# VectorE in place of GpSimd for weight and input splits of a hybrid decoder step, and a new order of TensorE's steps

## Chip, core and metric

The kernel runs on one core of one Trainium2 chip. The metric is the device time of one execution in microseconds; a comparison takes the median of several executions. The engines are named as in the profile: PE (TensorE, with its weight loads as PEld), DVE (VectorE), ACT (ScalarE), POOL (GpSimd), SP (SyncE, which issues most DMAs).

## What is computed

One layer of a decoder for a prompt of 512 rows and 8 single-row samples (520 columns in all once transposed), width 1024, all in float32:

```
h = rms_norm(x, g_mix)
proj = einsum('ntd,de->nte', h, w_in)                  # 5632 columns
u_a, z_b, u_c, gate_in = split(proj)                   # 1024, 1024, 512, 3 x 1024
c_a = causal_dwconv(u_a, width 4)                      # branch A: RG-LRU
y_a = linear_scan(a, sqrt(1 - a*a) * sigmoid(ig) * c_a)  # gates by 8 block-diagonal products
glu_b = z_b[:512] * sigmoid(z_b[512:])                 # branch B: Conformer convolution
y_b = silu(layer_norm(causal_dwconv(glu_b, width 31)))
y_c = s5_ssm(u_c)                                      # branch C: complex diagonal scan
y_c = gelu(y_c); y_c = y_c * sigmoid(y_c @ w_glu_c + b)
merged = g_a * (y_a @ w_pa) + g_b * (y_b @ w_pb) + g_c * (y_c @ w_pc)
x = x + merged @ w_out
x = x + (silu(gate) * up) @ w_ffn_out                  # gate, up = rms_norm(x) @ w_ffn_in
out = rms_norm(x, g_final), and the new states of all branches
```

## The kernel before

Activations lie transposed: 128 channels on the partitions, the 520 columns on the free axis in two halves of 260. Every large product is made from split operands: a float32 operand is divided into a high part (`hi`, rounded by ScalarE's copy) and a low part (`lo = x - hi`), and three products hi.hi, hi.lo, lo.hi are summed in PSUM (`prod`, L252). An output tile of 128 channels with 8 input tiles is therefore 48 TensorE instructions, one with 4 input tiles 24.

Weights come in by SP's DMAs of 1024 KB (two output tiles at a time, `wload`), two such buffers. `wsplit` makes `whi` on ScalarE (L226) and `wlo` by a subtraction (L227); there are three buffers of each, so the split for one product waits until the product three weights earlier is done. Which engine subtracts is a table: `eng(key)` gives GpSimd for the keys in ON_POOL and VectorE for the others. Weight keys are `w.<matrix>.<tile>`, for instance `w.in.23`; tiles 0 to 7 of w_in are step a, 8 to 11 b1, 12 to 15 b0, 20 to 27 ga, 28 to 35 gb, 36 to 43 gc. Other keys: `ac.t` the split of branch A's convolved input (in `a_conv`, helper `split`, L258 and L259), `ya.t` the split of its output, `yg.k` the split after the GELU, `wrg.t` that of the gate weights, `rot.t` and `unrot.t` the imaginary half of the rotations before and after the S5 scan (L917 to L919, L927 to L929), `eb`, `ca` (L840 to L848), `wt` (L810 to L820) tables of branch C, `caz`, `ebz` memsets, `hs.t` the 8 sample columns of the RG-LRU state (L1125 to L1131). ON_DVE does the same for `ca` and `wt`, whose default is GpSimd.

The order of the middle part is the string ORDER, written out by hand. Each word calls one step function: b0/b1 (branch B's two halves of the input product), a (branch A's), gc/ga/gb (the gates, stored to DRAM as g_d and loaded back), cp/cq/cr/cd/cm/ci/co (branch C: tables, transposes, products, scan, output), ac (branch A's width-4 convolution, L1057 to L1067), ag (its gate products, two tiles' weights fetched at every even one), ar (its recurrence, in pairs), bc (branch B's width-31 convolution), glu, pc/pa/pb (the three output projections), ln1 to ln3. TensorE executes in exactly this order. The other four engines' queues are laid out by the framework's scheduler from the same sequence, and each engine executes its queue in order. `b_low` emits branch B's convolution with a very low priority: its 29 multiply-adds per tile (L1229, two dependent chains `acc` and `odd`) fill VectorE's queue where nothing more urgent stands.

After ORDER follow w_out with the residual, the FFN in two halves, the last norm and the stores.

Of the kernel before, what the change touches and what calls it, by code (L numbers as in the profile page):

```python
# [29 lines left out]
DFF = 2816  # L30

ON_POOL = set("""
ac.0 ac.4 ac.6 ac.7 caz.0 caz.1 caz.2 eb.1 ebz.0 ebz.1 ebz.2 ebz.3 hs.0 hs.2 hs.3 hs.4 hs.5 hs.6 hs.7 rho.2
rot.1 rot.2 rot.3 unrot.3 w.glu.0 w.glu.1 w.glu.3 w.in.10 w.in.12 w.in.2 w.in.21 w.in.23 w.in.26 w.in.31 w.in.35
w.in.37 w.in.38 w.in.39 w.in.4 w.in.40 w.in.7 w.in.8 w.w_pa.1 w.w_pa.3 w.w_pa.4 w.w_pa.5 w.w_pa.7 w.w_pb.1
w.w_pb.2 w.w_pb.5 w.w_pb.7 w.w_pc.0 w.w_pc.2 w.w_pc.3 w.w_pc.5 w.w_pc.6 w.w_pc.7 wrg.6 ya.1 ya.2 yg.0 yg.3
""".split())

ON_DVE = set("""
ca.2 ca.3 wt.0 wt.1 wt.3  # L40
""".split())

CONV_PE = ()
AFTER3 = False

ORDER = """
b0.0 cp.0 as b0.1 ct ap s0 bs cp.1 b1.0 b1.1 cr.0 b0.2 cq.1 b0.3 ci.0 cr.1 gc.0 gc.1 cq.0 b1.2 cd.0 b1.3 cm.0 a.0 ci.1
a.2 ac.0 a.1 cd.1 a.3 a.4 ac.1 gc.2 co.0 cp.2 gc.3 cm.1 cr.2 ag.0 cq.2 co.1 cd.2 ag.1 ac.2 ci.2 a.5 cp.3 ac.3 gc.4
gc.5 cm.2 cr.3 co.2 cd.3 ag.2 ar.0 gc.6 gc.7 cq.3 ci.3 cm.3 ga.0 ga.1 ag.3 ga.6 ga.7 a.6 a.7 bc.0 ac.4 ac.5 ar.1 ga.2
ga.3 ag.4 ag.5 bc.1 ar.2 bc.2 ga.4 ga.5 co.3 gb.4 ac.6 gb.5 gelu ag.6 glu.0 glu.1 ac.7 glu.2 glu.3 gb.0 gb.1 ag.7 pc.0  # L50
pc.1 ar.3 pc.2 bc.3 pc.3 asp pc.4 pc.5 gb.2 pc.6 pc.7 gb.3 lnp pa.0 pa.1 pa.2 pa.3 ln1 gb.6 gb.7 ln2 pa.4 pa.5 pa.6
ln3 pa.7 pb.0 pb.1 pb.2 pb.3 pb.4 pb.5 pb.6 pb.7
"""


# [1576 lines left out]
```

## Time and profile before

| what | value |
|---|---|
| median of 3 runs | 929.35 us (928.15 to 930.03) |
| profiled execution | 928.63 us |
| its span, first to last instruction | 926.6 us |
| PE busy | 866.2 us, 93% of the span, 7329 instructions |
| DVE busy | 598.2 us, 65%, 942 |
| ACT busy | 355.1 us, 38%, 519 |
| POOL busy | 299.2 us, 32%, 363 |
| mean granted TensorE clock | 0.97 |
| weight splits on DVE (L227) | 113, 128.0 us |
| weight splits on POOL (L227) | 33, 77.7 us, mean 2355 ns |

Busy shares are averages over stages with different limits, so the table only says where to look. The views that decide are those of one stage: the busy time of each engine in a stretch, what an engine waited for there, and the mean of one instruction beside its undisturbed duration.

### The profile page before, as it was taken

The page shows a single profiled execution, that of the slowest core. Times are in us where ns is not written, and L with a number is a line of the kernel's source. Part 1 is how long each engine was busy: PE and PEld are TensorE (multiplying, and loading weights), DVE is VectorE, ACT ScalarE, POOL GpSimd, SP SyncE. Part 2 cuts the span into 40 slices and gives each one's busy share as a digit, 9 for nine tenths or more (in the row PEclk, how much of TensorE's full clock was granted, in tenths as well). Part 3 has the DMA queues.
Part 4 walks back from the last instruction along what each step waited for, and adds up shares of the span by engine and source line. Part 5 has one row for each costly group of instructions (what it writes and reads, how often), then busy time and mean ns, then how long its engine had stood idle before and what let it go on. Part 6 is the DMA issues. An engine that isn't in the chain of part 4 may idle for free.

```text
span 926.6 us, 17538 instructions
## 1 busy us (share of the span) xinstructions
PE 866.2 (93%) x7329; PEld 854.6 (92%) x7329; DVE 598.2 (65%) x942; ACT 355.1 (38%) x519; POOL 299.2 (32%) x363
## 2 busy tenths in 40 slices
PE   7879999979968589899999999999999999999997
PEld 6879999879968579799999999999999999999997
DVE  7897877797799999997784454444432234444443
ACT  6523243436466546334443443333221223333331
POOL 6558987746845754424311200000000000000021
PEclk9989999999998879899999999999999999999999
DMA  6921333232312304453454222322133432321322
GB/s 198 281 89 58 115 105 112 73 93 81 126 57 69 104 23 150 160 183 105 160 204 140 92 90 90 123 92 72 52 87 92 147 109 92 104 71 43 98 75 92
DMA packets 103630, 99.74 MB, mean 108 GB/s; under 512 B 8675, under 2 KB 94935, under 8 KB 103023
## 3 DMA queue, kind: packets, MB, share of 16 engines
q1 hardware_dynamic: 103215, 98.01, 32.4%
q8 instruction: 57, 0.93, 0.4%
q0 software_dynamic: 320, 0.57, 0.2%
q14 instruction: 22, 0.18, 0.1%
q10 hardware_dynamic: 16, 0.03, 0.0%
HBM read 86.57 MB, written 12.58 MB: 107 GB/s over the span
## 4 chain that ended last, share of the span: by engine, by line
PE 76%; DVE 16%; POOL 3%; issue 2%; ACT 1%; DMA 1%; SPq 0%; DVEq 0%; ACTq 0%; POOLq 0%
PE mm L252 69%; DVE t L1229 4%; PE mm L1581 3%; DVE q L1229 2%; DVE wlo L227 1%; PE mm L969 1%; DMA t<-w_ig 1%; DVE tx L1059 1%; DVE s_t L592 1%; PE mm L905 1%; DMA q<-x_prompt 1%; DVE s_n L601 1%; DVE h L259 1%; DVE q L1129 0%; POOL h L352 0%
## 5 line engine op out<-in xcount | busy, mean ns | idle before, releaser
L252 PE MATMUL mm<-q,whi 128*128 128x260 f32 x3296 | 420.4, 285 | 5.2 <-ACT t L138 2.3
L252 PEld LDWEIGHTS mm<-q,whi 128*128 128x128 f32 x3296 | 406.9, 190 | 7.2 <-ACT t L138 2.9
L227 DVE TENSOR_TENSOR wlo<-wraw,whi 128x1024 fp32r<-128x1024 f32 (+3 forms) x113 | 128.0, 1133 | 231.3 <-PE mm L252 130.4
L226 ACT ACTIVATE whi<-wraw 128x1024 fp32r<-128x1024 f32 (+3 forms) x146 | 139.4, 955 | 245.9 <-PE mm L252 213.1
L252 PE MATMUL mm<-q,wlo 128*128 128x260 f32 x1648 | 215.4, 282 | 0.0
L252 PEld LDWEIGHTS mm<-q,wlo 128*128 128x128 f32 x1648 | 204.5, 188 | 0.0
L1453 POOL TENSOR_TENSOR t<-t,t 128x260 f32<-128x260 f32 (+1 forms) x9 | 8.4, 931 | 370.5 <-ACT t L1451 370.5
L252 PE MATMUL mm<-h,whi 128*128 128x260 f32 x800 | 108.2, 290 | 4.4 <-DVE h L259 3.6
L252 PEld LDWEIGHTS mm<-h,whi 128*128 128x128 f32 x800 | 103.1, 196 | 5.4 <-DVE h L259 4.2
L227 POOL TENSOR_TENSOR wlo<-wraw,whi 128x1024 fp32r<-128x1024 f32 (+1 forms) x33 | 77.7, 2355 | 69.7 <-ACT whi L226 26.4
L1229 DVE SCALAR_TENSOR_TENSOR t<-q,vec,t 128x512 f32<-128x512 f32 x71 | 61.4, 883 | 0.0
L252 PE MATMUL mm<-h,wlo 128*128 128x260 f32 x400 | 57.1, 289 | 4.0 <-DVE wlo L227 4.0
L252 PEld LDWEIGHTS mm<-h,wlo 128*128 128x128 f32 x400 | 52.8, 194 | 4.3 <-DVE wlo L227 4.3
L138 ACT ACTIVATE t<-t,zero_t 128x520 f32<-128x520 f32 x30 | 21.5, 729 | 56.6 <-DVE t L1522 56.6
L252 PE MATMUL mm<-t,t 128*128 128x260 f32 x96 | 17.3, 338 | 24.8 <-ACT t L258 24.1
L252 PEld LDWEIGHTS mm<-t,t 128*128 128x128 f32 x96 | 15.2, 235 | 26.6 <-ACT t L258 25.0
L138 ACT ACTIVATE t<-mm,vec 128x520 f32<-128x520 f32 x44 | 30.0, 689 | 19.6 <-PE mm L252 16.5
L1229 DVE SCALAR_TENSOR_TENSOR q<-q,vec 128x512 f32<-128x512 f32 x30 | 31.0, 1035 | 0.0
L132 ACT ACT_TABLE_LOAD x22 | 28.2, 1283 | 1.1 <-PEq L1620 0.7
L258 ACT ACTIVATE h<-t 128x520 fp32r<-128x520 f32 x18 | 11.5, 636 | 43.8 <-DVE t L592 43.8
L1372 POOL TENSOR_TENSOR t<-t,t 128x520 f32<-128x520 f32 x7 | 9.2, 1318 | 50.0 <-ACT t L1371 50.0
L592 DVE TENSOR_TENSOR t<-t,t 128x520 f32<-128x520 f32 x30 | 20.8, 699 | 0.7
(424 smaller groups left out, 980.5 us busy)
## 6 DMA issues: line engine op xcount, KB each, us to landing
wraw<-w_ffn_in SPq DMA_DIRECT2D x22, 1024.0 KB
wraw<-w_in SPq DMA_DIRECT2D x20, 1024.0 KB
g_d<-t SPq DMA_DIRECT2D x24, 260.0 KB
t<-g_d SPq DMA_DIRECT2D x24, 260.0 KB
wraw<-w_ffn_out SPq DMA_DIRECT2D x16, 384.0 KB
wraw<-w_ffn_out SPq DMA_DIRECT2D x16, 320.0 KB
wraw<-w_pa SPq DMA_DIRECT2D x4, 1024.0 KB
wraw<-w_out SPq DMA_DIRECT2D x4, 1024.0 KB
```

The lines of the kernel that those rows point to most:

```text
L132: last_tab[0] = after(S.preload_act_table_set(SETS[func]), last_tab[0])
L138: last_tab[0] = after(S.activation(out, x, func, **kw), last_tab[0])
L226: S.activation(hi, raw, AF.Copy)
L227: e.tensor_tensor(lo, raw, hi.bitcast(F32), op=ALU.subtract)
L252: T.matmul(ps[:, h, 0:HN], w_, x[:, h * HN:(h + 1) * HN], start=first and i == 0, stop=last and i == n - 1)
L258: S.activation(hi, src, AF.Copy)
L259: e.tensor_tensor(lo, src, hi.bitcast(F32), op=ALU.subtract)
L592: V.tensor_tensor(out, x, y, op=ALU.mult)
L601: V.tensor_scalar(n_, n_, MG, None, op0=ALU.subtract)
L905: T.matmul(ps[:, q // 2, (q % 2) * 136:(q % 2) * 136 + 136], d["ebt"][:, ri, q, :], d["u4"][:, q, 8:144], start=True, stop=True)
L1229: ins = V.scalar_tensor_tensor(x, win(k), wdw(k, t), x, op0=ALU.mult, op1=ALU.add)
L1581: T.matmul(ps[:, 0, 0:HN], w[:, k, :], x[:, h * HN:(h + 1) * HN], start=j == 0 and k == 0 and i == 0, stop=j == 1 and k == hk - 1 and i == 2)
```

## The change

Two tables and the string are edited; no instruction's arithmetic changes. Twenty weight splits move from GpSimd to VectorE (w_in tiles 7, 12, 21, 23, 26, 31, 35, 37, 38; glu 0, 1; pa 1, 4, 7; pb 5; pc 2, 3, 5, 6, 7) and four the other way (w_in 36, w_out 3, pa 2, pb 4). ac.0, ac.4, ac.6, ac.7, ya.2, rot.2, rot.3, unrot.3, hs.3, hs.7 and three memsets (caz.0 to caz.2) move to VectorE, yg.2 and caz.3 to GpSimd. The tables ca.0 and wt.2 move to VectorE. In ORDER some 30 of 131 steps stand elsewhere: among them a.6 before ga.6 and ga.7, ac.4 before ci.3, bc.0 before a.6, bc.2 before ar.2, bc.3 right behind ag.6, co.3 right behind ag.5, and ga.4, ga.5 and ag.7 behind pc.1. Line numbers of the changed file are one lower from L52 on.

```
 ON_DVE = set("""
-ca.2 ca.3 wt.0 wt.1 wt.3
+ca.0 ca.2 ca.3 wt.0 wt.1 wt.2 wt.3
 """.split())
...
-gc.5 cm.2 cr.3 co.2 cd.3 ag.2 ar.0 gc.6 gc.7 cq.3 ci.3 cm.3 ga.0 ga.1 ag.3 ga.6 ga.7 a.6 a.7 bc.0 ac.4 ac.5 ar.1 ga.2
-ga.3 ag.4 ag.5 bc.1 ar.2 bc.2 ga.4 ga.5 co.3 gb.4 ac.6 gb.5 gelu ag.6 glu.0 glu.1 ac.7 glu.2 glu.3 gb.0 gb.1 ag.7 pc.0
+gc.5 cm.2 cr.3 co.2 cd.3 ag.2 ar.0 gc.6 gc.7 ag.3 cm.3 cq.3 ac.4 ci.3 ga.0 ga.1 bc.0 a.6 ga.6 ga.7 a.7 ac.5 ar.1 ga.2
+ga.3 ag.4 ag.5 co.3 bc.1 bc.2 ar.2 gb.4 ac.6 gb.5 gelu ag.6 bc.3 glu.0 glu.1 ac.7 glu.2 glu.3 gb.0 gb.1 pc.0 pc.1 ga.4
```

VectorE's queue where branch B's convolution begins, before. `wlo` is a weight split (here for a.6, then ga.2), L1202 to L1236 the sample columns of the convolution, L1229 its multiply-adds, L1061 and L1067 the end of ac.4, L1059 a part of ac.5:

```order
L227 TENSOR_TENSOR wlo_3262<-wraw_3259,whi_3261 128x1024
L227 TENSOR_TENSOR wlo_3471<-wraw_3468,whi_3470 128x1024
L1202 TENSOR_TENSOR t_3372<-q_801,vec 128x248
L1206 TENSOR_REDUCE t_3374<-t_3372 128x8
L1061 SCALAR_TENSOR_TENSOR t_3414<-q_804,vec,tx_3410 128x2x256
L1067 SCALAR_TENSOR_TENSOR t_3414<-q_804,vec,tx_3410 128x2x4
L1236 TENSOR_SCALAR t_3371<-t_3374,vec 128x2x4
L1229 SCALAR_TENSOR_TENSOR t_3371<-q_801,vec,t_3371 128x2x256
```

And in the changed kernel (L926 to L928 are unrot.3; the two splits are those for ga.7 and a.7):

```order
L927 TENSOR_TENSOR t_3016<-t_3010,h_2540 128x512
L591 TENSOR_TENSOR h_2996<-t_3011,h_2540 128x4x128
L926 TENSOR_TENSOR t_3015<-t_3011,h_2540 128x512
L226 TENSOR_TENSOR wlo_3313<-wraw_3254,whi_3312 128x1024
L1201 TENSOR_TENSOR t_3159<-q_801,vec 128x248
L924 TENSOR_TENSOR h_3009<-h_2996 128x4x128
L928 TENSOR_TENSOR h_3009<-t_3015,t_3016 128x4x128
L1205 TENSOR_REDUCE t_3161<-t_3159 128x8
L1235 TENSOR_SCALAR t_3158<-t_3161,vec 128x2x4
L226 TENSOR_TENSOR wlo_3369<-wraw_3197,whi_3368 128x1024
L1228 SCALAR_TENSOR_TENSOR t_3158<-q_801,vec,t_3158 128x2x256
```

The convolution's first multiply-add stood behind the split for ga.2 and now stands behind the one for a.7, two steps earlier in TensorE's order; unrot.3 and a.7's split, which were GpSimd's, stand ahead of it.

GpSimd's queue from the GELU to the w_pc products, before (L259 are the splits of ac.6, wrg.6, yg.0, yg.3, ac.7, ya.1, ya.2; L1118 multiplications of the recurrence; L227 the weight splits of glu and pc):

```order
L259 TENSOR_TENSOR t_3967<-t_3963,t_3966 128x520
L259 TENSOR_TENSOR t_4047<-t_4045,t_4046 128x512
L259 TENSOR_TENSOR h_4029<-q_607,h_4028 128x520
L259 TENSOR_TENSOR h_4031<-q_607,h_4030 128x520
L1118 TENSOR_TENSOR t_4069<-t_4069,t_3963 128x520
L227 TENSOR_TENSOR wlo_4195<-wraw_4158,whi_4194 128x512
L259 TENSOR_TENSOR t_4151<-t_4147,t_4150 128x520
L227 TENSOR_TENSOR wlo_4370<-wraw_4367,whi_4369 128x512
L259 TENSOR_TENSOR h_4568<-q_803,h_4567 128x520
L259 TENSOR_TENSOR h_4570<-q_803,h_4569 128x520
L227 TENSOR_TENSOR wlo_4468<-wraw_4465,whi_4467 128x512
L1118 TENSOR_TENSOR t_4358<-t_4358,t_4147 128x520
```

And in the changed kernel:

```order
L258 TENSOR_TENSOR t_3933<-t_3931,t_3932 128x512
L258 TENSOR_TENSOR h_3915<-q_607,h_3914 128x520
L258 TENSOR_TENSOR h_3917<-q_607,h_3916 128x520 x2
L1131 COPY fin_a<-q_804 128x1
L1117 TENSOR_TENSOR t_3955<-t_3955,t_3849 128x520
L1131 COPY fin_a<-q_804 128x1
L226 TENSOR_TENSOR wlo_4119<-wraw_4082,whi_4118 128x512
L226 TENSOR_TENSOR wlo_4276<-wraw_4273,whi_4275 128x512
L258 TENSOR_TENSOR h_4635<-q_803,h_4634 128x520
L1117 TENSOR_TENSOR t_4411<-t_4411,t_4071 128x520
```

The splits of ac.6, ac.7, ya.2 and of pc.2 are gone from it, and one more GELU split (yg.2) is in it.

## Rows read from the trace of the kernel before

**Rows 1.** Busy time by stretch: a:b, length, PE, PEld, DVE, ACT, POOL, PEclk, DMA, GB/s.
```profile
45.00:250.00 205.00, 193.34 (x1811) 188.03 (x1810) 160.84 (x316) 80.38 (x127) 149.78 (x220) 0.97 0.29 93
250.00:402.00 152.00, 119.53 (x981) 117.25 (x981) 149.66 (x191) 83.11 (x115) 79.16 (x58) 0.89 0.30 102
402.00:485.00 83.00, 83.00 (x687) 82.76 (x687) 68.08 (x78) 33.40 (x44) 24.97 (x13) 1.00 0.45 158
```
**Rows 2.** Timeline of PE at pa.0: start, length, engine, line, what.
```profile
402.06 4.00 PE L252 MATMUL mm<-h,whi 128*128 128x260 f32 x32
```
**Rows 3.** What PE waited for from 245 to 333 us: total, times, longest.
```profile
PE mm L252 <- ACT t L258: 21.2, 2, 11.4
PE mm L252 <- DVE h L259: 3.6, 1, 3.6
```
**Rows 4.** DVE by line and form, 250.2 to 402: busy us, mean ns, idle before.
```profile
L1229 DVE SCALAR_TENSOR_TENSOR t<-q,vec,t 128x512 f32<-128x512 f32 x66 | 57.7, 894 | 0.0
L1229 DVE SCALAR_TENSOR_TENSOR q<-q,vec 128x512 f32<-128x512 f32 x24 | 24.5, 1020 | 0.0
L1229 DVE SCALAR_TENSOR_TENSOR q<-q,vec,q 128x512 f32<-128x512 f32 x15 | 14.2, 946 | 0.2
L227 DVE TENSOR_TENSOR wlo<-wraw,whi 128x1024 fp32r<-128x1024 f32 x8 | 9.7, 1209 | 0.0
L1059 DVE SCALAR_TENSOR_TENSOR tx<-q,vec,tx 128x544 f32<-128x544 f32 x6 | 6.8, 1129 | 0.0
...
L227 DVE TENSOR_TENSOR wlo<-wraw,whi 128x512 fp32r<-128x512 f32 x3 | 2.0, 671 | 0.0
```
**Rows 5.** Line L1229: shortest, median, longest ns over the trace.
```profile
L1229 DVE SCALAR_TENSOR_TENSOR t<-q,vec,t x71: 718/740/2887, 250.3 to 414.3; 128x512 f32<-128x512 f32 x71
```
**Rows 6.** Timeline, 252 to 258 us, DVE and POOL.
```profile
252.87 2.83 POOL L227 TENSOR_TENSOR wlo<-wraw,whi 128x1024 fp32r<-128x1024 f32 x1
253.38 2.91 DVE L1059 SCALAR_TENSOR_TENSOR tx<-q,vec,tx 128x544 f32<-128x544 f32 x1
...
257.54 0.77 DVE L1059 SCALAR_TENSOR_TENSOR tx<-q,vec,tx 128x544 f32<-128x544 f32 x1
```
**Rows 7.** POOL by line and form, 250.2 to 402.
```profile
L227 POOL TENSOR_TENSOR wlo<-wraw,whi 128x512 fp32r<-128x512 f32 x9 | 20.1, 2236 | 14.3 <-issue 9.1 <-ACT whi L226 4.2 <-PE mm L252 0.9
L259 POOL TENSOR_TENSOR t<-t,t 128x520 fp32r<-128x520 f32 x3 | 11.2, 3748 | 9.5 <-ACT t L258 9.5
L227 POOL TENSOR_TENSOR wlo<-wraw,whi 128x1024 fp32r<-128x1024 f32 x3 | 8.8, 2926 | 7.4 <-ACT whi L226 7.4
...
L259 POOL TENSOR_TENSOR h<-q,h 128x520 fp32r<-128x520 f32 x4 | 6.6, 1658 | 2.9 <-ACT h L258 2.9
L1118 POOL TENSOR_TENSOR t<-t,t 128x520 f32<-128x520 f32 x4 | 5.8, 1449 | 1.2 <-ACT t L138 1.2
```
**Rows 8.** Timeline: PE's last products of ag.3; DVE where the convolution begins.
```profile
233.78 1.47 PE L252 MATMUL mm<-t,t 128*128 128x260 f32 x11
...
246.84 1.57 DVE L227 TENSOR_TENSOR wlo<-wraw,whi 128x1024 fp32r<-128x1024 f32 x1 [4.99 <-PE mm L252]
...
250.30 3.15 DVE L1229 SCALAR_TENSOR_TENSOR t<-q,vec,t 128x512 f32<-128x512 f32 x3
```
**Rows 9.** DVE by line, 45 to 250.2: the group with most idle before it.
```profile
L227 DVE TENSOR_TENSOR wlo<-wraw,whi 128x1024 fp32r<-128x1024 f32 x16 | 21.3, 1332 | 21.2 <-PE mm L252 11.2 <-ACT whi L226 9.9
```
**Rows 10.** What PE waited for from 160 to 210 us.
```profile
PE ms L859 <- DVE h L789: 3.0, 1, 3.0
```
**Rows 11.** Timeline, 270 to 282 us: a weight split's high part, then ag.4's gate weights.
```profile
270.65 1.06 ACT L226 ACTIVATE whi<-wraw 128x1024 fp32r<-128x1024 f32 x1
...
280.43 0.63 ACT L258 ACTIVATE t<-t 128x512 fp32r<-128x512 f32 x1 [6.62 <-DMA t<-w_ig]
281.09 0.69 DVE L259 TENSOR_TENSOR t<-t,t 128x512 fp32r<-128x512 f32 x1 [1.70 <-ACT t L258]
```
**Rows 12.** Timeline: PE at glu.0.
```profile
332.71 2.94 PE L252 MATMUL mm<-h,whi 128*128 128x260 f32 x10 [3.56 <-DVE h L259]
```

More of the change, by code (lines that the diff above doesn't have):

```diff
@@ L32 @@
 ON_POOL = set("""
[L33 to L36, printed above, removed]
+caz.3 eb.1 ebz.0 ebz.1 ebz.2 ebz.3 hs.0 hs.2 hs.4 hs.5 hs.6 rho.2 rot.1 w.glu.3 w.in.10 w.in.2 w.in.36 w.in.39 w.in.4
+w.in.40 w.in.8 w.w_out.3 w.w_pa.2 w.w_pa.3 w.w_pa.5 w.w_pb.1 w.w_pb.2 w.w_pb.4 w.w_pb.7 w.w_pc.0 wrg.6 ya.1 yg.0 yg.2
+yg.3
 """.split())
 ON_DVE = set("""
-ca.2 ca.3 wt.0 wt.1 wt.3
+ca.0 ca.2 ca.3 wt.0 wt.1 wt.2 wt.3
 """.split())
@@ L46 @@
 ORDER = """
-b0.0 cp.0 as b0.1 ct ap s0 bs cp.1 b1.0 b1.1 cr.0 b0.2 cq.1 b0.3 ci.0 cr.1 gc.0 gc.1 cq.0 b1.2 cd.0 b1.3 cm.0 a.0 ci.1
-a.2 ac.0 a.1 cd.1 a.3 a.4 ac.1 gc.2 co.0 cp.2 gc.3 cm.1 cr.2 ag.0 cq.2 co.1 cd.2 ag.1 ac.2 ci.2 a.5 cp.3 ac.3 gc.4
-gc.5 cm.2 cr.3 co.2 cd.3 ag.2 ar.0 gc.6 gc.7 cq.3 ci.3 cm.3 ga.0 ga.1 ag.3 ga.6 ga.7 a.6 a.7 bc.0 ac.4 ac.5 ar.1 ga.2
-ga.3 ag.4 ag.5 bc.1 ar.2 bc.2 ga.4 ga.5 co.3 gb.4 ac.6 gb.5 gelu ag.6 glu.0 glu.1 ac.7 glu.2 glu.3 gb.0 gb.1 ag.7 pc.0
-pc.1 ar.3 pc.2 bc.3 pc.3 asp pc.4 pc.5 gb.2 pc.6 pc.7 gb.3 lnp pa.0 pa.1 pa.2 pa.3 ln1 gb.6 gb.7 ln2 pa.4 pa.5 pa.6
-ln3 pa.7 pb.0 pb.1 pb.2 pb.3 pb.4 pb.5 pb.6 pb.7
+b0.0 cp.0 as b0.1 ct s0 bs cp.1 b1.0 b1.1 cr.0 b0.2 b0.3 cq.1 ci.0 cr.1 gc.0 gc.1 b1.2 cd.1 cd.0 b1.3 a.0 cq.0 cm.0
+ci.1 a.2 a.1 a.3 ac.1 gc.2 a.4 ac.0 cp.2 co.0 gc.3 cd.2 cm.1 ap ag.0 cq.2 co.1 ac.2 cr.2 ag.1 ci.2 a.5 cp.3 ac.3 gc.4
+gc.5 cm.2 cr.3 co.2 cd.3 ag.2 ar.0 gc.6 gc.7 ag.3 cm.3 cq.3 ac.4 ci.3 ga.0 ga.1 bc.0 a.6 ga.6 ga.7 a.7 ac.5 ar.1 ga.2
+ga.3 ag.4 ag.5 co.3 bc.1 bc.2 ar.2 gb.4 ac.6 gb.5 gelu ag.6 bc.3 glu.0 glu.1 ac.7 glu.2 glu.3 gb.0 gb.1 pc.0 pc.1 ga.4
+ag.7 ga.5 ar.3 pc.2 pc.3 pc.4 pc.5 asp gb.2 pc.6 pc.7 gb.3 lnp pa.0 pa.1 pa.2 pa.3 ln1 gb.6 gb.7 ln2 pa.4 ln3 pa.5
+pa.6 pa.7 pb.0 pb.1 pb.2 pb.3 pb.4 pb.5 pb.6 pb.7
 """
```

## Prediction

> **What bounds the kernel now.** Read the stages first [rows 1]. From 45 to 250 us TensorE (PE) is busy 193.34 of 205 us and VectorE (DVE) 160.84, so TensorE sets the pace and VectorE has 44.2 us to spare. From 250 to 402 us it is the other way round: VectorE is busy 149.66 of 152 us, TensorE only 119.53, at a granted clock of 0.89. From 402 to 485 us TensorE is busy 83.00 of 83 us, and behind that stand w_out and the FFN, of which the change moves one split. So the stretch up to the first w_pa product, pa.0, which starts at 402.06 us [rows 2], is what can move.
>
> Then ask what TensorE waits for in the middle [rows 3]: 21.2 us in two waits, for ScalarE rows that themselves stand behind VectorE work, and 3.6 us for a VectorE split directly. They are one lateness, met at several steps: VectorE's queue is too long.
>
> Then ask what fills that queue. The depthwise convolution (L1229) is 66+24+15 instructions with means of 894, 1020 and 946 ns [rows 4], but the median of the first form, over its 71 in the whole trace, is 740 ns and its longest is 2887 [rows 5]. The timeline shows why [rows 6]: the same L1059 instruction takes 2.91 us beside a weight split that runs on GpSimd (POOL) and 0.77 us four microseconds later, when GpSimd runs no tensor_tensor. A long GpSimd tensor_tensor stops one VectorE instruction for a while; VectorE pays for work that it was spared.
>
> **What one GpSimd instruction costs VectorE.** Over the stretch, mean against undisturbed: 66 x (894-740) = 10.2 us, 24 x (1020-740) = 6.7, 15 x (946-740) = 3.1, the six L1059 6 x (1129-770) = 2.2; 22.2 us, a lower bound, since the smaller groups are left out. On the other side stand GpSimd's long instructions [rows 7]: 9 of 512 columns, 3+4+4 of 520 and 3 of 1024; counted in units of about 512 columns 9+11+6 = 26. That is 0.85 us a unit at least; the pair in [rows 6] shows 2.91-0.77 = 2.14 for a split of two units, 1.07 each. I take **1.0 us a unit**, between the two. It can't be less than nothing, nor more than such an instruction itself takes, 1.45 us (the L1118 rows of [rows 7]).
>
> By the Trainium skill's page "SBUF — State Buffer" (section "A bandwidth-pool intuition that's wrong (but worth ruling out)") two such operations don't share a bandwidth: one is blocked until the other ends. By that rule a unit would cost the whole of GpSimd's time, the upper bound of 1.45, and the gain would be 7.2 us larger; the pair says 1.07, so the trace agrees with a block and not with its length, and the sum stays with 1.0.
>
> **The change, part by part.**
>
> *The middle stretch.* Off GpSimd go seven 512-column splits (glu.0, glu.1, pc.2, pc.3, pc.5, pc.6, pc.7), three of 1024 (in.23, in.31, pa.1), the input splits ac.4, ac.6 and ac.7, and ya.2; yg.2 comes the other way. Units: 7+6+4-1 = 16, relief 16.0 us. VectorE's own price, duration less about 0.08 us by which neighbours overlap (1.21 for 1024 and 0.67 for 512 columns [rows 4], 0.69 for 520 [rows 11]): 3 x 1.13 + 7 x 0.59 + 3 x 0.61 = 9.35 us. **Net 6.65 us less** in a queue that has no idle time. Bounds: no relief makes it 9.35 us more, 1.45 a unit 13.9 us less.
>
> *The start of the convolution.* It begins at 250.30 us, behind the split for ga.2, for which VectorE stood idle 4.99 us until TensorE had done ga.7 [rows 8]. In the new order it stands behind the split for a.7, whose buffer comes free when a.6 is done, and a.6 now follows directly on the steps that end with ag.3 today, at 235.25 us [rows 8]. With a step of 48 products at 48 x 83.00/687 = 5.8 us [rows 1], ScalarE's part at 1.06 [rows 11] and the split at 1.21, that is 243.3 us: up to 7.0 us earlier, if VectorE has done what stands ahead. Ahead of it VectorE gets five splits of 1024 net (in.12, 37, 38, 21, 26 and 7 come, in.36 goes): 5.65 us; rot.2, rot.3 and unrot.3 with three instructions each, wt.2 with six, and ac.0: 16 x 0.61 = 9.8; ca.0 with eight smaller ones at half that, 2.6. Together 18.1 us, less a relief of up to 10+16+4 = 30 units if all collided and nothing if none did. Of the 44.2 us idle there, 21.2 are splits that wait for TensorE's pace [rows 9], a wait that shrinks as VectorE gets later. So I let this cover hide the 18.1 us. Where the cover fails is known: TensorE waits 3.0 us for c_pool's rows there now (L789 [rows 10]), and that would grow first. I take **5 us earlier**, between 7 and a loss of 2.
>
> *New or kept waits.* The gate weights of ag.4 are still fetched only when GpSimd's small state copies have freed their tile: then comes a DMA that ScalarE waits 6.62 us for, and 1.70 us of VectorE idle [rows 11]. hs.4 stays on GpSimd, so this chain stays; with the shorter queue VectorE waits more there, some 3 us. The split for pc.3 now waits for ga.4, which stands only three steps ahead of it: about 1 us. Together **2.1 us worse** than now.
>
> *TensorE's order.* ga.4 and ga.5 move from before co.3 to behind pc.1. They are fillers of 5.8 us each; moved, they leave TensorE less to do before ag.6 and glu.0, and more behind. From glu.0 to pa.0 TensorE then has 12 steps of 24 products, 6 of 48 and one pair of gates: 34.8+34.8+1.4 = 71 us. For pa.0 at 392.6 glu.0 must run from 321.6 on. Its last wait ends today at 332.71 us [rows 12], 11 us too late; but that time holds the 11.6 us of ga.4 and ga.5, and VectorE's share of the gain, so this fits with a few us to spare. I cost it at nothing; without that room pa.0 is late by what is missing.
>
> *Everything else.* SP's queue moves with the steps (weights and gates are issued at the same distance ahead). pa.2, w_out.3 and pb.4 go to GpSimd, and pa.4, pa.7, pb.5 and w.in.35 leave it, all behind pa.0, where TensorE has no gap and a split has three buffers of room: nothing. Memsets (caz) and two small hs groups: nothing, under 0.5 us each.
>
> **Sum:** 6.65 + 5 - 2.1 = 9.5 us. The profiled execution took 928.63 us (span 926.6 and 2.0 around it), so 919.1; the median of the three runs is 0.7 us above it, and I give **919.5 us**.
>
> **Rivals.**
>
> *Nothing gained (924 to 931).* The 18.1 us ahead of the convolution are not hidden: waits as that at L789 grow by some 5 to 7 us, the convolution starts at 250 as now or later, and the 6.65 us less new waits are all but used up: 928.6 - 6.65 + 2.1 + 3 = about 927. For it: idle of a queue that waits for the right moments is not free idle. Against: 44.2 us of it, half of them waits for pace. 0.20.
>
> *Slower (931 to 940).* VectorE is the fullest engine of the stretch and the change gives it 9.35 us more of its own. If the ten units that stay on GpSimd there simply meet other VectorE rows, with longer waits each, the relief is small; below 9.35/16 = 0.58 us a unit the stretch gets longer. With none: 928.6 + 9.35 = 938. For it: the median in [rows 5] is undisturbed, so a stop is not the rule for every row. Against: the means in [rows 4] and the pair in [rows 6]. 0.13. The Trainium skill's page "Perfetto Trace Analysis" (section "Optimizing Scalar/DVE Operations") has the rule for this rival: with VectorE saturated, giving work to GpSimd may pay; it adds that the two share a port and it might not. The trace agrees with the second half.
>
> *More gained (903 to 914).* Relief of 1.45 a unit, the convolution at 243, and TensorE's wait in [rows 10] gone, since three rotations no longer run on GpSimd: 928.6 - 13.9 - 7 - 3 = 904.7, and less than all of it is likelier than all. 0.17.
>
> That the change doesn't do what it says is out: the built queues show the instructions moved.
>
> **How the numbers follow.** Forecast (914 to 924) 0.50, nothing 0.20, slower 0.13, more 0.17. Range 906 to 932: it leaves out half of the slower case and the tail of the larger gain. A measurement here can tell 0.2%, 1.9 us. Faster by more than that: 0.50 + 0.17 + 0.07 of the second case = 0.74; within 0.10; slower 0.16.
>
> **What would show it.** Right: L1229's means in the stretch near 800 ns or less; its first instruction near 245 us; pa.0 near 392; from there to the end the same 524 us. Wrong: L1229's means unchanged (the unit price), the first L1229 at 250 or later with a longer wait at L788 (the cover), or VectorE with idle time in the stretch and TensorE waiting all the same (a new wait).

## The result and the profile after

The changed kernel takes 917.58 us (median of 4 runs, 915.97 to 917.74) where the kernel before takes 929.0 in the same comparison: ratio 0.9873, 95% interval 0.9856 to 0.9890. The profiled execution took 915.97 us (its span 913.8 us), 12.66 us less than the profiled one of before.

Busy time by stretch in the changed kernel (a:b, length, PE, PEld, DVE, ACT, POOL, PEclk, DMA, GB/s), cut at the first convolution instruction and at pa.0 as [rows 1] are:

```profile
45.00:243.70 198.70, 182.16 (x1728) 178.40 (x1727) 170.73 (x346) 79.45 (x127) 113.20 (x192) 0.95 0.29 92
...
243.70:389.50 145.80, 123.74 (x1037) 122.01 (x1035) 142.47 (x208) 83.72 (x114) 43.73 (x37) 0.89 0.34 112
...
389.50:913.80 524.30, 517.22 (x4305) 515.79 (x4303) 251.83 (x320) 165.30 (x221) 41.28 (x29) 1.00 0.32 104
```

GpSimd's busy time in the middle falls from 79.16 to 43.73 us; VectorE is nearly as full as before (142.47 of 145.80 us), in a stretch that is 6 us shorter. The last row is the part behind pa.0: 524.30 us, where before it was 926.6 - 402.06 = 524.54. So all of the gain lies ahead of pa.0, which the timelines of PE and DVE place:

```profile
389.50 1.24 PE L251 MATMUL mm<-h,whi 128*128 128x260 f32 x9
...
242.89 1.22 DVE L226 TENSOR_TENSOR wlo<-wraw,whi 128x1024 fp32r<-128x1024 f32 x1
244.02 5.38 DVE L1228 SCALAR_TENSOR_TENSOR t<-q,vec,t 128x512 f32<-128x512 f32 x8
```

pa.0 starts at 389.50 instead of 402.06 [rows 2], 12.56 us earlier; the convolution at 244.02 instead of 250.30 [rows 8], 6.3 us earlier. The stretch between the two is 145.5 us instead of 151.8.

VectorE's convolution (three rows) and GpSimd's long instructions (the rows behind the "...") by line and form in that stretch, with busy us, mean ns, idle before; they answer to [rows 4] and [rows 7]:

```profile
L1228 DVE SCALAR_TENSOR_TENSOR t<-q,vec,t 128x512 f32<-128x512 f32 x71 | 54.9, 801 | 0.0
L1228 DVE SCALAR_TENSOR_TENSOR q<-q,vec 128x512 f32<-128x512 f32 x18 | 16.2, 903 | 0.1
...
L1228 DVE SCALAR_TENSOR_TENSOR q<-q,vec,q 128x512 f32<-128x512 f32 x15 | 11.1, 737 | 0.0
...
L1117 POOL TENSOR_TENSOR t<-t,t 128x520 f32<-128x520 f32 x4 | 10.6, 2658 | 18.3 <-ACT t L137 18.3
L258 POOL TENSOR_TENSOR h<-q,h 128x520 fp32r<-128x520 f32 x4 | 7.0, 1772 | 6.0 <-ACT h L257 6.0
...
L226 POOL TENSOR_TENSOR wlo<-wraw,whi 128x512 fp32r<-128x512 f32 x2 | 3.0, 1520 | 9.1 <-PE mm L251 7.7 <-ACT t L1225 1.4
```

The convolution's means fall from 894, 1020 and 946 ns to 801, 903 and 737, beside an undisturbed 740: fewer GpSimd instructions, fewer stops. What TensorE still waits for from 243 to 317 us (total, times, longest):

```profile
PE mm L251 <- ACT t L257: 16.3, 2, 8.2
PE mm L251 <- POOL t L258: 2.9, 1, 2.9
PE mm L251 <- DVE h L258: 2.2, 1, 2.2
```

These are the same places as in [rows 3], ag.4, ag.6 and glu.0, and the waits for ScalarE and VectorE are each shorter; the one for GpSimd, at ag.6, has grown from 0.57 us. From glu.0 at 316.29 to pa.0 TensorE waits only 0.7 us. In 160 to 210 us the picture turned: the wait for c_pool's rows [rows 10] is gone, and the gate products of ag.0 and ag.2, the two groups there, wait 9.3 us instead of 2.9.

### The profile page after: what moved, and what is told of

Its sections match the earlier page's. It is cut to its first block, busy times and chain, and to the rows that moved or that the text cites. A ratio compares the mean times of both kernels' runs of the same rounds, so it can differ in the third digit from the quotient of the medians.

```text
span 913.8 us, 17525 instructions
## 1 busy us (share of the span) xinstructions
PE 860.5 (94%) x7329; PEld 851.3 (93%) x7329; DVE 598.2 (65%) x993; ACT 355.2 (39%) x519; POOL 224.2 (25%) x312
## 4 chain that ended last, share of the span: by engine, by line
PE 75%; DVE 13%; ACT 3%; POOL 3%; issue 2%; DMA 2%; SPq 1%; DVEq 0%; ACTq 0%; POOLq 0%
PE mm L251 69%; PE mm L1580 3%; DVE t L1228 3%; DVE wlo L226 2%; SPq L198 1%; DMA t<-w_ig 1%; ACT t L137 1%; PE mm L968 1%; DMA wraw<-w_in 1%; DVE q L1228 1%; DMA q<-x_prompt 1%; DVE t L418 1%; DVE t L591 0%; DVE tx L1058 0%; PE mm L904 0%
## 5 line engine op out<-in xcount | busy, mean ns | idle before, releaser
L226 DVE TENSOR_TENSOR wlo<-wraw,whi 128x1024 fp32r<-128x1024 f32 (+3 forms) x129 | 145.0, 1124 | 215.8 <-PE mm L251 115.8
L251 PE MATMUL mm<-h,whi 128*128 128x260 f32 x800 | 106.1, 287 | 2.9 <-DVE h L258 2.9
L251 PEld LDWEIGHTS mm<-h,whi 128*128 128x128 f32 x800 | 101.2, 192 | 3.5 <-DVE h L258 3.4
L1228 DVE SCALAR_TENSOR_TENSOR t<-q,vec,t 128x512 f32<-128x512 f32 x71 | 54.9, 801 | 0.0
L226 POOL TENSOR_TENSOR wlo<-wraw,whi 128x1024 fp32r<-128x1024 f32 (+1 forms) x17 | 36.4, 2142 | 70.8 <-PE mm L251 53.0
L251 PE MATMUL mm<-t,t 128*128 128x260 f32 x96 | 19.7, 378 | 28.5 <-ACT t L257 25.6
L251 PEld LDWEIGHTS mm<-t,t 128*128 128x128 f32 x96 | 17.8, 276 | 29.7 <-ACT t L257 26.5
L1117 POOL TENSOR_TENSOR t<-t,t 128x520 f32<-128x520 f32 x8 | 16.4, 2047 | 45.2 <-ACT t L137 45.2
```

The source lines that it names most:

```text
L226: e.tensor_tensor(lo, raw, hi.bitcast(F32), op=ALU.subtract)
L251: T.matmul(ps[:, h, 0:HN], w_, x[:, h * HN:(h + 1) * HN], start=first and i == 0, stop=last and i == n - 1)
L1117: G.tensor_tensor(ig, ig, c, op=ALU.mult)
L1228: ins = V.scalar_tensor_tensor(x, win(k), wdw(k, t), x, op0=ALU.mult, op1=ALU.add)
```

## Experiments

A "stop" is the time by which a VectorE instruction takes longer than it does undisturbed. Theory (price): a long GpSimd tensor_tensor stops VectorE about 1.0 us per 512 columns, which is more than VectorE needs to do the work itself. Rivals: TensorE's new order does it; GpSimd's results came late; VectorE's own load decides. One measurement here tells 0.2%, 1.9 us.

### Tables or order

Order only: the changed kernel with ON_POOL and ON_DVE of before.

```
 ON_DVE = set("""
-ca.0 ca.2 ca.3 wt.0 wt.1 wt.2 wt.3
+ca.2 ca.3 wt.0 wt.1 wt.3
```

> The changed kernel with the three tables of before, so only TensorE's order is new. Price theory (a long GpSimd instruction costs VectorE about 1.0 us per 512 columns, more than doing it): the middle's relief of 6.65 us is lost and the earlier start of the convolution is kept, so about 923 to 925 us, the convolution's means between 250 and 400 us back near 890 to 1000 ns, its first instruction near 245. Order theory (the new order does it all, the tables nothing): 917 to 919. Tables theory (the order does nothing): 928 to 930.

Measured: 933.56 us, ratio to before 1.0047 (1.0029 to 1.0065). Slower, and none of the three theories had this: the order by itself costs 4 to 5 us.

Tables only: the kernel before with the changed tables; ORDER is the one of before.

> The kernel before with the tables of the change, so only who does the splits is new. Price theory: the convolution starts near 250 us as before, its means fall to about 800 ns, pa.0 some 5 us earlier, so 922 to 925 us. Order theory: 928 to 930. Tables theory: 917 to 919.

Measured: 918.35 us, ratio 0.9892 (0.9868 to 0.9915), not to be told from the whole change (0.9873). That is the range of the tables theory; the price theory had 922 to 925. So the tables are the gain, 10 us in the old order and 933.56 - 917.58 = 16 us in the new one. VectorE's row from 217 us to the convolution's start shows what the order does (order only, tables only, the change; columns as above):

```profile
217.00:249.40 32.40, 32.40 (x273) 32.40 (x272) 32.08 (x36) 15.87 (x22) 26.98 (x27) 1.00 0.22 71
```
```profile
217.00:246.50 29.50, 29.50 (x249) 29.50 (x249) 21.36 (x36) 11.86 (x17) 15.37 (x17) 1.00 0.47 153
```
```profile
217.00:244.00 27.00, 27.00 (x228) 27.00 (x228) 26.82 (x43) 14.49 (x21) 13.10 (x23) 1.00 0.30 103
```

In the new order VectorE has no idle time there (32.08 of 32.40, 26.82 of 27.00): the start is set by VectorE's own queue, and it comes at 249.4 while GpSimd does 26.98 us beside it, at 244.0 when it does 13.10. In the old order VectorE has 8.1 us to spare, in two waits for buffers that TensorE still reads, and a still lighter table, further down, gives the same start, 246.5. The order moves the limit from TensorE to VectorE; only the tables make use of it.

### Undoing one half of the tables

The middle back: in the changed kernel, fourteen instructions between the convolution's start and pa.0 return to GpSimd and one goes the other way, 16 units net. The lines here and in the next experiments are the keys that ON_POOL gains (+) and loses (-).

```
+ac.4 ac.6 ac.7 ya.2 w.in.23 w.in.31 w.glu.0 w.glu.1 w.w_pa.1 w.w_pc.2 w.w_pc.3 w.w_pc.5 w.w_pc.6 w.w_pc.7
-yg.2
```

> The changed kernel with the 16 units of the middle stretch given back to GpSimd (weight splits in.23, in.31, glu.0, glu.1, pa.1, pc.2, 3, 5, 6, 7; input splits ac.4, 6, 7; ya.2; yg.2 goes to VectorE). Price theory: 9.35 us of VectorE work leaves, 16 us of stops come: 6.65 us longer, 923 to 925 us, unless TensorE's own chain behind glu.0 hides a part (then 920 to 922). Order theory: 917 to 919. A theory that VectorE's own load is what counts: 9 us shorter, 908 to 910.

Measured: 927.43 us (10 runs), 9.85 us longer than the change and 2.4 above the range expected. VectorE has 9.35 us less of its own to do and the kernel is 9.85 us longer: that puts a unit at (9.35 + 9.85)/16 = 1.2 us, if all of the difference were stops; the table of VectorE's time below puts it at 1.0. The convolution's means, from its start to pa.0, go back towards the 894, 1020 and 946 ns of before:

```profile
L1228 DVE SCALAR_TENSOR_TENSOR t<-q,vec,t 128x512 f32<-128x512 f32 x71 | 57.9, 842 | 0.0
L1228 DVE SCALAR_TENSOR_TENSOR q<-q,vec 128x512 f32<-128x512 f32 x24 | 25.2, 1050 | 0.3
L1228 DVE SCALAR_TENSOR_TENSOR q<-q,vec,q 128x512 f32<-128x512 f32 x15 | 13.3, 884 | 0.1
```

The early part back: the moves ahead of the convolution are undone.

```
+ac.0 rot.2 rot.3 unrot.3 w.in.7 w.in.12 w.in.21 w.in.26 w.in.37 w.in.38
-w.in.36
 ON_DVE = set("""
-ca.0 ca.2 ca.3 wt.0 wt.1 wt.2 wt.3
+ca.2 ca.3 wt.0 wt.1 wt.3
```

> The changed kernel with the moves ahead of the convolution undone (weight splits in.12, 37, 38, 21, 26, 7, the rotations rot.2, rot.3, unrot.3, the tables ca.0 and wt.2, and ac.0 on GpSimd again; in.36 on VectorE again). Cover theory (VectorE's 18.1 us there are hidden, and the start of the convolution is set by the order): first convolution instruction within 1.5 us of 244.0, 916 to 919 us. Rival (the start moved because GpSimd was late ahead of it): it starts near 249, 922 to 924 us.

Measured: 927.38 us (10 runs), 9.80 us longer; the convolution starts at 249.3. My expectation failed, and its rival was right about the start, though not about the time (922 to 924). The start accounts for 5.3 of the 9.80 us; the rest arises behind it, where VectorE is idle and stopped some 2 us more each. The timeline of DVE and POOL shows what returns: a product of rot.3, then one of unrot.3, on GpSimd beside VectorE's scan of 1.2 us.

```profile
235.87 1.77 POOL L918 TENSOR_TENSOR t<-t,t 128x512 f32<-128x512 f32 x1 [1.93 <-DVE t L913]
...
236.41 2.31 DVE L921 TENSOR_TENSOR_SCAN t<-t,t 128x512 f32<-128x512 f32 x1
...
241.08 1.74 POOL L927 TENSOR_TENSOR t<-t,h 128x512 f32<-128x512 f32 x1
...
241.60 2.31 DVE L921 TENSOR_TENSOR_SCAN t<-t,t 128x512 f32<-128x512 f32 x1
```

In the changed kernel the two scans take 2.33 us together, here 2.31 each:

```profile
234.73 2.33 DVE L921 TENSOR_TENSOR_SCAN t<-t,t 128x512 f32<-128x512 f32 x2
```

The halves, 9.85 + 9.80 = 19.65 us, come to more than the 16 us of undoing all tables, so the two are not independent.

### The price by itself

In the changed kernel GpSimd has idle time ahead of the convolution's start. Eight instructions that nobody waits for are put there:

```
+        for _ in range(8 if t == 5 else 0):
+            G.tensor_tensor(uext[1][:, 0, 0:512], a_st[4][0][:, 0:512], a_st[4][0][:, 0:512], op=ALU.mult)
         split(c, chh, chl, eng(f"ac.{t}"))
```

> The changed kernel with eight more GpSimd tensor_tensors of 512 columns (two inputs from SBUF), behind ac.4's convolved input and ahead of the convolution's start, where GpSimd has 10 us of idle time; they write a region that nothing reads again, and the queues of all other engines are the same row for row. Price theory (a GpSimd tensor_tensor stops VectorE about 1.0 us per 512 columns): VectorE is full there, so the first convolution instruction comes some 8 us later (252 instead of 244), and the end 5 to 8 us later, 922 to 926 us. Lateness theory (what cost time before was that GpSimd's own results came late, not that it stopped VectorE): nothing waits for these eight, so 916 to 919 us.

In the second run the line is `G.tensor_copy(uext[1][:, 0, 0:512], a_st[4][0][:, 0:512])`.

> The same eight instructions as copies, with one input instead of two, all else the same. If any long GpSimd instruction stops VectorE: first convolution instruction near 252 and 922 to 926 us. If it takes two inputs: 244 and 916 to 919 us. In the trace of the changed kernel GpSimd's small copies stand beside VectorE instructions of ordinary length, which speaks for the second.

In the third the second input is another tile, `a_st[4][2][:, 0:512].bitcast(F32)`, with a subtraction.

> The run with eight added GpSimd tensor_tensors, but with two different input tiles in place of one tile taken twice, as the splits have; all other queues the same. There a stop was about 0.75 us (conv 5.7 us later for eight), beside splits 1.05. If two different inputs make the difference: the convolution starts 8 us later than in the changed kernel (252) and the time is 924 to 926 us; if not: 249.7 and 922 to 924 us.

| eight added | us (changed kernel 917.58) | convolution starts | GpSimd's own, median | stop of one VectorE row |
|---|---|---|---|---|
| copies | 919.35 | 247.3 | 1.10 us | 0.35 us |
| tensor_tensor, one tile twice | 922.96 | 249.7 | 1.48 us | 0.79 us |
| tensor_tensor, two tiles | 926.77 | 254.1 | 1.74 us | 1.04 us |

The stop is read from L1058, undisturbed 0.77 us (timelines of the three runs in this order, the last with the VectorE row before it and the GpSimd row beside it):

```profile
235.33 1.12 DVE L1058 SCALAR_TENSOR_TENSOR tx<-q,vec,tx 128x544 f32<-128x544 f32 x1
```
```profile
232.50 1.56 DVE L1058 SCALAR_TENSOR_TENSOR tx<-q,vec,tx 128x544 f32<-128x544 f32 x1
```
```profile
232.84 0.73 DVE L917 TENSOR_TENSOR t<-h,h 128x512 f32<-128x512 f32 x1
232.98 1.73 POOL L1072 TENSOR_TENSOR q<-t,t 128x512 f32<-128x512 f32 x1
233.49 1.81 DVE L1058 SCALAR_TENSOR_TENSOR tx<-q,vec,tx 128x544 f32<-128x544 f32 x1
```

In each run every one of the eight stops exactly one VectorE row: the copies by 0.25 to 0.46 us, one tile taken twice by 0.74 to 0.85, two tiles by 1.04 to 1.11 (each against the shortest tenth of its line and shape).

Work that nothing depends on makes the kernel longer by 5.4 and 9.2 us, and TensorE's and VectorE's own waits for GpSimd are no longer than in the changed kernel; so lateness of GpSimd's results is ruled out as the mechanism here, and the price is measured: 8 x 1.04 = 8.3 us of the 9.2 for the form that the splits have. The copies fit neither of the two expectations: they stop VectorE too, for a third of that; 1.8 us in the median is at the limit of what a measurement here tells, but the start moves 3.3 us. The Trainium skill's page "SBUF — State Buffer" (section "Who interferes with whom") has two inputs from SBUF on VectorE's side contend with any GpSimd instruction that reads SBUF; the trace agrees, the copies included. Its lock for the whole instruction shows as well: the stopped row ends 0.59 us after the GpSimd row beside it (235.30 and 234.71 us), so most of its 0.77 us of work is done after that. The price is all the same less than GpSimd's duration, 1.04 of 1.74 us: the VectorE row before it still ran at its ordinary 0.73 us while the GpSimd row had already begun. "GPSIMD Engine Reference" (section "2.1 Instruction dispatch") of the Trainium skill puts a two-input loop at about 2.5 cycles an element, at its 1.2 GHz an estimate of 1.07 us for 512 columns, close to the stop.

### Further in the same direction

Most of the rest of GpSimd's long work up to pc.0 on VectorE (rot.1 stays): seven splits of 1024 columns, two of 512, five input splits, and L1117.

```
-w.in.2 w.in.4 w.in.8 w.in.10 w.in.36 w.in.39 w.in.40 w.glu.3 w.w_pc.0 yg.0 yg.2 yg.3 ya.1 wrg.6
...
-            G.tensor_tensor(ig, ig, c, op=ALU.mult)
+            tmul(ig, ig, c)
```

> The changed kernel with the rest of the long GpSimd work up to pc.0 on VectorE too: weight splits in.2, 4, 8, 10, 36, 39, 40, glu.3, pc.0; yg.0, 2, 3, ya.1, wrg.6; and the recurrence's multiplication by c. Price theory: seven 1024-column splits gain 2.1 - 1.1 = 1.0 us each, the shorter ones 0.4 each, and TensorE's wait of 2.9 us for GpSimd's wrg.6 goes: up to 12 us where VectorE is full, half of that where it is not; 907 to 912 us. Rival (VectorE's own load now delays TensorE at the steps with three buffers of room): 918 to 925 us.

And the same tables in the order of before:

> The same tables in TensorE's order of before. If the order does nothing once the tables are new, the time is that of the run before this one within 2 us; if the new order is what makes room for VectorE's load, it is 3 to 6 us slower.

Measured: 908.14 us (ratio to before 0.9779, 0.9758 to 0.9799) in the new order, 1.0% under the change and the fastest kernel here; 915.71 (0.9858, 0.9840 to 0.9877) in the old one, 7.6 us slower where I had expected 3 to 6. With hardly a long GpSimd instruction left beside them, all 71 rows of the convolution's first form in the new order are undisturbed (shortest, median, longest ns, as in [rows 5]):

```profile
L1227 DVE SCALAR_TENSOR_TENSOR t<-q,vec,t x71: 712/739/750, 234.1 to 353.0; 128x512 f32<-128x512 f32 x71
```

VectorE's row from 217 us to the start, new order and old:

```profile
217.00:234.10 17.10, 17.10 (x145) 17.10 (x145) 17.01 (x28) 7.94 (x11) 4.39 (x8) 1.00 0.25 84
```
```profile
217.00:246.50 29.50, 29.50 (x249) 29.50 (x249) 21.93 (x36) 11.84 (x16) 14.11 (x16) 1.00 0.47 153
```

With a still shorter queue the convolution starts at 234.1 in the new order and stays at 246.5 in the old. The worth of the order goes from -4.8 us with the old tables over nothing to +7.6.

One wait taken away: all small state steps (hs) of the RG-LRU on VectorE, in the changed kernel.

> The changed kernel with all small RG-LRU state steps (hs.0, 2, 4, 5, 6) on VectorE too. In the chain of waits of the changed kernel two of them on GpSimd (2.34 and 1.72 us at 269.6) stand ahead of the copy that frees the tile for ag.4's gate weights. If that chain bounds ag.4: its gate products start 3 to 4 us earlier (274 to 275 instead of 278.1), VectorE's wait of 3.04 us there goes, and the time is 914 to 916 us. If VectorE's queue is what counts and its wait there is only borrowed: 917 to 919 us.

Measured: 917.13 us, no difference that can be told. The wait went (VectorE no longer waits at ag.4, whose gate products begin at 276.41 us instead of 278.13), and nothing came of it; VectorE has fifteen small instructions more.

At last the same, rot.1 and three w_pa splits on top of the 908.14 us kernel:

> The fastest kernel so far (the rest of the long GpSimd work on VectorE, 908.14 us) with hs.0, 2, 4, 5, 6, rot.1 and the splits pa.2, 3, 5 on VectorE as well. Price theory: rot.1's three instructions and three 1024-column splits gain 0.2 to 1.0 us each where VectorE is full, ag.4 comes 3 us earlier: 903 to 907 us. If VectorE is already so short of room that TensorE waits for it: 908 to 911 us.

Measured: 909.41 us (0.9796, 0.9781 to 0.9810), not to be told from 908.14: the end of this road.

### What the time of VectorE is made of

From 45 us to ln1's first product (425.1 us in the run before, 412.5 in the change) VectorE's time divides into idle time (length less busy time), stops (for each instruction its duration less that of the shortest tenth of the same source line and shape over all the traces) and the rest, its own work. In us:

| | length | idle | stops | own work | median of runs |
|---|---|---|---|---|---|
| before | 380.1 | 48.0 | 78.1 | 254.0 | 929.0 |
| order only | 384.5 | 45.1 | 82.5 | 256.9 | 933.56 |
| tables only | 366.9 | 32.9 | 53.5 | 280.5 | 918.35 |
| the change | 367.5 | 32.9 | 53.7 | 280.9 | 917.58 |
| further, old order | 365.5 | 42.7 | 25.0 | 297.8 | 915.71 |
| further, new order | 354.4 | 33.2 | 23.8 | 297.4 | 908.14 |

The change adds 26.9 us of work to VectorE; 24.4 us of it come back as stops that no longer happen, and 15.1 from idle time, so 12.6 us are gained. Over the whole stretch, then, the stops alone do not pay for the work. The same division ahead of the convolution's start (from 45 us) and behind it (to ln1) shows where they do; middle back and early back are the two experiments above, the profiled execution of the first being the slowest of its ten, 930.12 us (idle, stops, own work in us; sums can differ from the table above by 0.2):

| | ahead of the start | behind it |
|---|---|---|
| before | 44.2, 44.5, 116.6 | 3.9, 33.5, 137.4 |
| order only | 37.5, 48.3, 118.6 | 7.6, 34.2, 138.4 |
| the change | 28.0, 36.4, 134.7 | 4.9, 17.2, 146.3 |
| middle back | 32.8, 35.1, 132.7 | 7.4, 33.6, 139.9 |
| early back | 32.5, 52.3, 119.5 | 6.8, 19.3, 147.1 |

Behind the start, where VectorE is full, the stops are 33.5 to 34.2 us with the middle's 16 units on GpSimd and 17.2 or 19.3 without: about 1.0 us a unit, more than VectorE's own 8.9 us of extra work. Ahead of it the change adds 18.1 us of work for 8.1 us fewer stops, and idle time pays the larger part. Before 217 us idle time pays all of it (VectorE is busy 133.25 us there before and 144.22 after, with the same stops, 34.3 and 34.8 us); from there to the start it had little to give (the rows of before, then of the change):

```profile
45.00:217.00 172.00, 160.34 (x1535) 155.03 (x1533) 133.25 (x287) 65.45 (x108) 121.80 (x190) 0.96 0.28 89
217.00:250.30 33.30, 33.30 (x281) 33.30 (x280) 27.89 (x33) 14.94 (x21) 27.99 (x30) 1.00 0.36 116
```
```profile
45.00:217.00 172.00, 155.47 (x1504) 151.70 (x1503) 144.22 (x304) 64.96 (x107) 100.10 (x169) 0.94 0.29 90
```

Further on in the first table the stops pay again (29.9 against 16.5 of work), and there the idle time depends on the order. From ln1 to the span's end it is 501.3 to 501.7 us in the first four rows, but 503.3 and 506.7 in the last two: of the 13.1 us that the 908.14 us kernel gains up to ln1, 5.4 are given back right behind it, where TensorE waits for VectorE (2.36 us) and its first 32 products take 6.78 us instead of about 4. After this wait and one of 1.55 us just before it, the granted clock stood at the lower of its two levels, 1.2 GHz, for 6.83 us; the mean of these products is 0.54, that of the ones behind them 1.00 (timeline of PE, then the stretches of both in the columns of [rows 1]):

```profile
402.89 6.78 PE L250 MATMUL mm<-q,whi 128*128 128x260 f32 x32 [2.36 <-DVE t L1308]
...
411.41 4.01 PE L250 MATMUL mm<-q,whi 128*128 128x260 f32 x32
```
```profile
402.89:409.50 6.61, 6.61 (x32) 6.61 (x33) 5.22 (x7) 1.24 (x2) 1.63 (x1) 0.54 0.03 9
411.41:415.25 3.84, 3.84 (x34) 3.84 (x33) 0.00 (x0) 0.69 (x1) 2.39 (x1) 1.00 0.20 72
```

## Why the prediction was right, and where it was not

919.5 us were forecast and 917.58 measured. Point by point:

- **What bounds, and where.** Right: VectorE's queue in the middle, and nothing behind pa.0 (524.30 us beside 524.54).
- **The price of a unit, 1.0 us.** Right where VectorE is full: 1.04 us measured by itself, 16.3 us fewer stops for 16 units behind the convolution's start, 1.2 at most from undoing the middle. The term of 6.65 us less the new waits, 4.55, stands as the 6.3 us by which the stretch got shorter; undone by itself it is 9.85. The slower rival needed less than 0.58 a unit and is out; the rule that was named for it, "Perfetto Trace Analysis" of the Trainium skill (section "Optimizing Scalar/DVE Operations"), is borne out in its second half: giving work to GpSimd did not help a full VectorE.
- **The convolution 5 us earlier.** The size was near (6.3), the cause was only half right, and that the size came out is luck. The step that failed is "So I let this cover hide the 18.1 us". The work was as large as forecast (from 116.6 to 134.7 us). To hide it and start 5 us earlier as well, the idle time would have had to give 23.1 us; it gave 16.2. Of the 44.2 us, 38.8 lay ahead of 217 us, and there the cover held: idle time fell by 11.0 us for 10.6 us of new work. From 217 us to the start VectorE had only 5.4 us of 33.3 to spare, nearly all of it the one wait of 4.99 us [rows 8] that the order takes away. There nothing was left to hide in, and 7.4 us of new work were paid by stops, which fell from 10.1 to 1.6 us. That is the relief that I had written down ("a relief of up to 10+16+4 = 30 units") and left out of the sum. Nor does the order set the start: alone it brings it to 249.4, 0.9 us earlier, and makes the kernel slower. Undoing the early moves costs 9.80 us where I gave them nothing, with 15.2 us less work and 15.9 us more stops ahead of the start. The cover was counted too large and the relief at nothing, two errors that cancelled.
- **TensorE's order at nothing.** Right for the moved fillers: glu.0 ran from 316.29 us, ahead of the 321.6 that it needed, and from there to pa.0 TensorE waited 0.7 us. For the order as a whole the result is nothing too (918.35 without it, 917.58 with it), but its value hangs on the tables.
- **New waits, 2.1 us.** At ag.4 VectorE waits 3.04 us (before 1.70), as said; none for pc.3. Taking that wait away gained nothing. Why stays open: up to ln1 VectorE's own work grew by only 0.9 us in that run, its idle time by 2.7.
- **The L789 wait "would grow first".** It went; ag.0 and ag.2 wait longer instead (9.3 us for 2.9), and still ag.2's products begin at 205.27, before at 206.20.
- **The arithmetic.** Two small slips: eight instructions at half of 0.61 us are 2.4, not 2.6, and 919.1 and 0.7 are 919.8, not 919.5. Neither changes anything.

Open: why the order alone is slower. Its VectorE is idle 2.9 us less than before, stopped 4.4 us more and has 2.9 us more work up to ln1. On TensorE the loss first stands at ag.4, whose gate products begin 7.0 us later than before, with the convolution started 0.9 us earlier (order only, then before):

```profile
288.12 5.50 PE L252 MATMUL mm<-t,t 128*128 128x260 f32 x24 [15.94 <-ACT t L258]
```
```profile
281.11 4.69 PE L252 MATMUL mm<-t,t 128*128 128x260 f32 x24 [11.36 <-ACT t L258]
```

Their weights were fetched from 283.31 us on, before from 277.57. No run took apart why.

## What to carry to other kernels

Work given to GpSimd is not free for VectorE: price it by the stop it causes, read as the mean of a VectorE line less its median or by adding instructions that nobody waits for, and, where VectorE is full, give it back when the stop exceeds VectorE's own duration. Idle time of a full-looking queue covers new work only where that idle time lies, so read it by short stretches up to the point that the work must precede. A new order and a new division of work are tried together and apart: here one decided whether the other was a loss, nothing or 7.6 us.

## What was not expected of the hardware

A GpSimd copy of 512 columns, with one input, stops VectorE as well (0.35 us), a tensor_tensor on one tile taken twice 0.79 us and one on two tiles 1.04 us, of GpSimd durations of 1.10, 1.48 and 1.74 us. The stopped row ends only after the GpSimd row has ended.
